# Decay products of the two widest levels as one 128-column product per head, and 128-row products for the low-rank gate, in a hybrid decoder step

## The chip, the core and the metric

The kernel runs on one core of a Trainium2 chip. A core has five engines that work in parallel: TensorE (PE, matrix products; its weight loads are listed as PEld), VectorE (DVE), ScalarE (ACT), GpSimd (POOL) and SyncE (SP, here the queue that issues most transfers). Data lies in HBM, is moved by DMA into SBUF (128 partitions), and products land in PSUM, from where VectorE or ScalarE read them. The metric is the device time of one execution in microseconds (us), as the median of several runs. Before the change it is 1834.86 us (three runs, 1833.53 to 1837.37).

## The reference, cut to what matters

One layer of a decoder trunk for a prompt of 256 tokens and 8 single-token samples. A combined input projection feeds three branches: spatial gating (A), a gated linear recurrence of 8 heads (B, "HGRN2") and one of 4 heads (C, "GLA"). They are merged, projected, and followed by an MLP. Both recurrences are computed by the same function; the decays of C come from a projection of rank 16:

```python
def step(S, inp):
    qc, kc, vc, lc = inp
    b = jnp.cumsum(lc, axis=1)
    diff = b[:, :, None] - b[:, None, :]
    decay = jnp.exp(jnp.where(causal, diff, -jnp.inf))
    att = jnp.einsum('bthd,bshd,btshd->bhts', qc, kc, decay)
    o = jnp.einsum('bhts,bshv->bthv', att, vc) + ...

log_a = jax.nn.log_sigmoid(glr @ p['gla_w_up'][l] + p['gla_b_up'][l]) / GLA_TAU
```

So `att[t, s]`, for s before t, is a sum over the 128 channels d of q[t,d] k[s,d] exp(b[t,d] - b[s,d]), where b is the running sum of the log decays. `glr` has 16 columns, `gla_w_up` is 16 by 512.

## The kernel before

**The main stream.** Nearly all of TensorE's work is the projections. `linear` (L716) runs `granule` (L649) over the weight's row blocks: 512 KB of weights are loaded by SyncE (L616), split by ScalarE into a rounded high part (`whi`, L109) and by VectorE into the rest (`wlo`, L106), and each 128 by 128 block is used in three products, L659, L660 and L661, with 264 columns (256 prompt tokens and 8 samples). The split runs two blocks ahead, into six buffers.

**The background.** The mixers' own work is cut into steps by Python generators (`mixer_a`, `mixer_r`, `samples_r`). After each granule `background` (L699) lets them go on by as much as a rate allows; a generator yields after each step, and `yield READY` holds it until the next granule. So TensorE's order, written out by hand in program order, is: 24 main products, then whatever small products the generators have reached. `slot` (L666) collects the products of the narrow levels (L679, 128 small ones at most) and of the samples' states (L686), and the steps of the conditioning projection (L376). The order on VectorE and ScalarE in this part is chosen by the scheduler of the framework.

**The recurrence (`mixer_r`, L1121).** It runs three times, for groups of four heads: twice for B, once for C. For a group, channels lie on partitions and heads and tokens along the free axis: q, k and the running sum c are [128, 4 heads, 264]. Decays are handled by levels: for a level of width m, the tokens are cut in pieces of 2m; within a piece the first half gives the s side and the second half the t side, and exp(b[t] - b[s]) is written as a product of two factors, both relative to the sum at the end of the first half. The levels 16 to 1 go through `slot` in blocks of 32 tokens. The two widest, m = 32 and m = 64, are a loop of their own (L1186). For such a level a tile `e` ([128, 4, 264], from the pool `blkp`) holds the t-side factors in `es` and the s-side factors in `ef`, interleaved as the tokens are. They are made by an exponential (L1192), a subtraction (through the helper at L106), an exponential (L1195) and two multiplications (helper L100). Then, after a `READY`, for each head and each half of the prompt (`hf`, 128 tokens) one product (L1208) takes all 128 columns of `e` in that half as the stationary operand, s side and t side alike, and the 64 t-side columns as the moving one. The result is [128, 8, 64] in one PSUM bank (`sm`). ScalarE then copies the useful blocks into `att` (L1211 and L1212 for m = 32, L1214 for m = 64); `att` is [128, 8, 128], indexed by twice the head plus the half.

After the loop come the products between the two halves (L1232: `kd` and `qd`, four heads, 128 by 128 by 128), transposes (L1239), the new states (L1248, L1249) and the outputs (L1271 to L1274).

**The samples' states (`samples_r`).** POOL issues the loads of the states (L1077) and of broadcast value rows (L1083); ScalarE scales a state (L1103), VectorE adds the new value (L1105), and POOL issues the store (L1106).

**The low-rank gate (`gla_group`, L1029).** A tile `wl` of 16 partitions holds `gla_w_up` (`wup`, 512 columns) and the 16 rows `lr` of the input projection (264 columns). The weights come by a POOL transfer (L1035), `lr` is copied by ScalarE out of the accumulator (L1043), and four products (L1048) with 16 rows each, one after each piece of the value projection, give the gate's inputs; VectorE adds the bias (L1049).

Of the kernel before, what the change touches and what calls it, by code (L numbers as in the profile page):

```python
# [15 lines left out]
P = 128  # L16
D = 2048
KT = D // P
NP = 256
NS = 8  # L20
NT = NP + NS
# [36 lines left out]
def hybrid_step_kernel(  # L58
# [8 lines left out]
    nc = tc.nc  # L67
    V, S, T = nc.vector, nc.scalar, nc.tensor
# [13 lines left out]
    def nm(s):  # L82
        uid[0] += 1
        return f"{s}_{uid[0]}"

    def blk(shape=None, dt=F32):
        shape = shape or [P, 4, NT]
        return blkp.tile(shape, dt, tag="b", name=nm("b"))

    def sm(shape=None):  # L90
        return psm.tile(shape or [P, 512], F32, tag="sm", name=nm("sm"))
# [4 lines left out]
    def const(shape, name, dt=F32):  # L96
        return cp.tile(shape, dt, tag=name, name=name)

    def mul(o, a, b):
        V.tensor_tensor(o, a, b, op=ALU.mult)  # L100

    def add(o, a, b):
        V.tensor_tensor(o, a, b, op=ALU.add)  # L103

    def sub(o, a, b):
        V.tensor_tensor(o, a, b, op=ALU.subtract)  # L106
# [56 lines left out]
    ps = sm()  # L163
# [120 lines left out]
    ps = sm([P, P])  # L284
# [431 lines left out]
    def linear(w, k0, nk, c0, width, xh, xl):  # L716

        acc = new_acc()
        kc = min(nk, 1024 // width)
        for kb in range(0, nk, kc):  # L720
            granule(w, k0, kc, c0, width, [acc], xh, xl, kb, kb == 0, kb + kc == nk)
            background()
        return acc[:, 0:width // P, 0:NT]
# [4 lines left out]
    def pair(b, g):  # L728
        return b[:, 2 * g:2 * g + 2, :]
# [9 lines left out]
    def zin(c0, width=CW):  # L739
        return linear(win, 0, KT, c0, width, hH, hL)  # L740
# [69 lines left out]
    for ci, n in enumerate(CHUNKS):  # L810
# [5 lines left out]
        for gi in range(ng):  # L816
# [5 lines left out]
            for acc, (c0, dst, fn) in zip(accs, begin[gi * gn:gi * gn + gn]):  # L822
                z = acc[:, :, 0:NT]
# [150 lines left out]
    def log_sigmoid(out, z, a):  # L974

        S.activation(a, z, AF.Abs)
        yield
        S.activation(a, a, AF.Exp, scale=-1.0)
        yield 1.6
        S.activation(a, a, AF.Ln, bias=1.0)  # L980
        yield 1.8
        V.scalar_tensor_tensor(out, z, 0.0, a, ALU.min, ALU.subtract)
        yield


    att = const([P, 8, P], "att")
# [42 lines left out]
    def gla_group():  # L1029
        G = Group()  # L1030
        G.dv, G.i = 256, 2
        G.q, G.g, G.k, G.v = blk(), blk(), blk(), [blk(), blk()]
        wl = blk([16, 512 + NT])
        wup, lr = wl[:, 0:512], wl[:, 512:512 + NT]
        nc.gpsimd.dma_start(wup, gla_w_up[0])  # L1035
        for s in range(2):
            z = zin(6144 + s * CW)
            S.copy(pair(G.q, s), z)
        for s in range(2):
            z = zin(6656 + s * CW)  # L1040
            S.activation(pair(G.k, s), z, AF.Copy, scale=GLA_SCALE)
        z = zin(9216, P)
        S.copy(lr, z[0:16, 0, :])  # L1043
        for s in range(4):
            z = zin(7168 + s * CW)
            S.copy(pair(G.v[s // 2], s % 2), z)
            ps = sm()
            T.matmul(ps[:, 0:NT], wup[:, s * P:(s + 1) * P], lr, start=True, stop=True)  # L1048
            V.tensor_scalar(G.g[:, s, :], ps[:, 0:NT], bupT[:, s:s + 1], None, ALU.add)  # L1049
        G.s_in = lambda b, h, n: state_gla[0, b, h:h + n].rearrange("h k v -> k h v")  # L1050
        G.s_out = lambda b, h, n: gla_sample[0, b, h:h + n].rearrange("h k v -> k h v")
        G.p_out = lambda h, n: gla_prompt[0, 0, h:h + n].rearrange("h k v -> k h v")

        def gates():
            yield from log_sigmoid(G.g, G.g, blk())
            V.tensor_scalar(G.g, G.g, 1.0 / GLA_TAU, None, ALU.mult)
            yield

        G.gates = gates
        return G  # L1060
# [60 lines left out]
    def mixer_r(G):  # L1121
# [4 lines left out]
        def v4(b, w):  # L1126
            return b[:, :, 0:NP].rearrange("p h (n j) -> p h n j", j=w)
# [17 lines left out]
        c = g  # L1145
# [13 lines left out]
        for li, m in enumerate(LEVELS):  # L1159
            n = NP // (2 * m)  # L1160
            yield lambda: len(levels) < LEVELS_HELD
            e = blk()
            ev, cv = v4(e, 2 * m), v4(c, 2 * m)
            ef, es = ev[:, :, :, 0:m], ev[:, :, :, m:2 * m]
# [16 lines left out]
        for b in range(4):  # L1181
            r = slice(32 * b, 32 * b + 32)
# [3 lines left out]
        for m in (32, 64):  # L1186
            n = NP // (2 * m)
            e = blk()
            ev, cv = v4(e, 2 * m), v4(c, 2 * m)
            ef, es = ev[:, :, :, 0:m], ev[:, :, :, m:2 * m]  # L1190
            mid = cv[:, :, :, m - 1:m].to_broadcast([P, 4, n, m])
            S.activation(es, cv[:, :, :, m:2 * m], AF.Exp)  # L1192
            sub(ef, mid, cv[:, :, :, 0:m])
            yield
            S.activation(ef, ef, AF.Exp)  # L1195
            mul(es, es, v4(q, 2 * m)[:, :, :, m:2 * m])
            yield
            mul(ef, ef, v4(k, 2 * m)[:, :, :, 0:m])
            add(cv[:, :, :, m:2 * m], cv[:, :, :, m:2 * m], mid)
            yield  # L1200

            yield READY
            ps = sm([P, 8, 64])
            for h in range(4):
                for hf in range(2):
                    b = e[:, h, P * hf:P * hf + P]
                    rhs = b.rearrange("p (n j) -> p n j", j=2 * m)[:, :, m:2 * m]
                    T.matmul(ps[:, 2 * h + hf, :].rearrange("p (n j) -> p n j", j=m), b, rhs, start=True, stop=True)  # L1208
            yield
            if m == 32:  # L1210
                S.copy(att[0:32, :, 32:64], ps[0:32, :, 0:32])  # L1211
                S.copy(att[64:96, :, 96:128], ps[64:96, :, 32:64])  # L1212
            else:
                S.copy(att[0:64, :, 64:128], ps[0:64])  # L1214

        cv = v4(c, P)
        kd, qd = blk([P, 4, NP]), blk([P, 4, P])
# [12 lines left out]
        ps = sm([P, 4, P])  # L1230
# [5 lines left out]
        for hf in range(2):  # L1236
            ps = sm([P, 4, P])
# [27 lines left out]
        for hf in range(2):  # L1265
            for h0 in range(0, 4, nh):
                ps = sm([P, nh, dv])
                for i in range(nh):
                    h = h0 + i
# [7 lines left out]
                for i in range(nh):  # L1277
                    h = h0 + i
# [10 lines left out]
        for j in range(nj):  # L1289
            for h2 in range(2):  # L1290
                ps = sm([P, 2, NP])
# [19 lines left out]
    for i in range(2):  # L1311
        Gs.append(hg_group(i))
        gens.append(mixer_r(Gs[i]))
        bg.g.append(gens[i])
    rate[:] = RATES[0]
    Gs.append(gla_group())
    gens.append(mixer_r(Gs[2]))
    bg.g.append(gens[2])

# [160 lines left out]
    for m in range(8):  # L1480
        if m in PRE_AT:
            n = N_PRE // len(PRE_AT)
            for _ in range(n):
                pre.load(True)
        z = linear(w_out[0], 0, KT, m * CW, CW, mH, mL)
# [29 lines left out]
    ps = sm([P, 2, KT, NS])  # L1515
# [178 lines left out]
    for t in range(2):  # L1694
        for hf in range(2):
# [8 lines left out]
            if t == 0 and hf == 0:  # L1704
# [3 lines left out]
                ps = sm([P, P])  # L1708
# [52 lines left out]
```

## Time and profile before

| what | before |
|---|---|
| median of three runs | 1834.86 us (1833.53 to 1837.37) |
| the profiled execution | 1832.18 us |
| its span, first to last instruction | 1830.4 us |
| mean granted TensorE clock | 0.997 |
| records of TensorE (PE) | 17012 |
| L659, L660, L661 together | 3850.9 us of overlapping durations, 13872 records |
| L1208 | 96 records, 434 to 716 us |
| L1048 | 8 records, 366 to 409 us |
| HBM traffic | 427.60 MB read, 11.70 MB written |

How to read the profile: times are microseconds from the span's start. A product of fp32 operands appears as two PE records and two PEld records, a main product as one of each. A record's duration overlaps that of the next, since matmuls are pipelined; the pace is the distance between starts. In a list of groups, "128\*128 128x64 f32 x96" is the size of the stationary operand, the output and the number of records. In a timeline, a bracket at the end gives the time the engine was idle before the instruction and what released it; "issue" there means that the profile shows nothing that it waited for.

### The profile page before, as it was taken

How to read it: one execution, taken by the hardware profiler on the slowest of the kernel's cores; microseconds unless marked ns; L12 is line 12 of the kernel's file. 1: busy time of each engine (PE TensorE's matmuls, PEld its weight loads, DVE VectorE, ACT ScalarE, POOL GpSimd, SP SyncE). 2: the span in 40 equal slices, each digit the busy share in tenths (PEclk: the TensorE clock that was granted, in tenths of full speed). 3: DMA queues.
4: the chain of work that ended last, by engine and by line, in shares of the span. 5: the costliest groups of instructions: out<-in, count | busy, mean ns of one | idle time of the engine just before them, and what ended most of it. 6: DMA issues, size and time to landing. Idle time of an engine off the chain costs nothing.

```text
span 1830.4 us, 42186 instructions
## 1 busy us (share of the span) xinstructions
PE 1788.7 (98%) x17012; PEld 1696.5 (93%) x17012; DVE 1181.8 (65%) x2092; ACT 1000.3 (55%) x1818; POOL 131.3 (7%) x210
## 2 busy tenths in 40 slices
PE   6999999999999999999999999999999999999998
PEld 4889999989988999989999989999999999999997
DVE  4566677787576696566555667555666666666666
ACT  5544364666755765654445666555554545454544
POOL 4221000111111101210000000000000000000000
PEclk9999999999999999999999999999999999999999
DMA  9999697788787788897987964777666666666663
GB/s 326 354 343 304 195 304 231 215 266 276 239 287 233 229 270 278 274 323 250 308 254 265 327 180 146 246 256 227 191 197 194 197 194 196 195 195 196 196 196 106
DMA packets 330179, 442.05 MB, mean 242 GB/s; under 512 B 14946, under 2 KB 276944, under 8 KB 329984
## 3 DMA queue, kind: packets, MB, share of 16 engines
q1 hardware_dynamic: 311728, 380.26, 65.0%
q0 software_dynamic: 17184, 57.85, 9.1%
q8 instruction: 133, 2.18, 0.5%
q10 hardware_dynamic: 1072, 1.25, 0.2%
q14 instruction: 62, 0.51, 0.1%
HBM read 427.60 MB, written 11.70 MB: 240 GB/s over the span
## 4 chain that ended last, share of the span: by engine, by line
PE 88%; DMA 2%; DVE 2%; issue 1%; ACT 1%; POOL 0%; DVEq 0%; ACTq 0%; POOLq 0%
PE mm L659 27%; PE mm L661 26%; PE mm L660 26%; PE ada L376 3%; DMA vbc<-vs_d 1%; PE ada L308 1%; DVE wlo L106 1%; PE sm L851 1%; PE sm L1208 1%; PE sm L679 1%; PE sm L686 1%; DMA raw<-in_w_in_dram 0%; DVE b L106 0%; PE sm L1578 0%; ACT whi L109 0%
## 5 line engine op out<-in xcount | busy, mean ns | idle before, releaser
L659 PE MATMUL mm<-b,whi 128*128 128x264 f32 x4624 | 1292.4, 279 | 12.3 <-issue 5.1
L661 PE MATMUL mm<-b,wlo 128*128 128x264 f32 x4624 | 1279.7, 277 | 5.1 <-DVE wlo L106 4.5
L660 PE MATMUL mm<-b,whi 128*128 128x264 f32 x4624 | 1278.8, 277 | 0.8 <-DVE b L106 0.7
L106 DVE TENSOR_TENSOR wlo<-raw,whi 128x512 fp32r<-128x512 f32 x1136 | 774.4, 689 | 489.1 <-ACT whi L109 475.0
L109 ACT CAST whi<-raw 128x512 fp32r<-128x512 f32 x1136 | 691.8, 616 | 644.5 <-DVE wlo L106 331.7
L659 PEld LDWEIGHTS mm<-b,whi 128*128 128x128 f32 x4624 | 875.8, 189 | 53.0 <-issue 28.0
L661 PEld LDWEIGHTS mm<-b,wlo 128*128 128x128 f32 x4624 | 876.2, 189 | 7.3 <-DVE wlo L106 7.2
L660 PEld LDWEIGHTS mm<-b,whi 128*128 128x128 f32 x4624 | 876.2, 189 | 4.4 <-issue 3.0
L103 DVE TENSOR_TENSOR b<-b,mm 128x528 f32<-128x528 f32 (+1 forms) x137 | 95.7, 699 | 24.5 <-PE mm L661 13.0
L1105 DVE SCALAR_TENSOR_TENSOR st<-vbc,b,st 128x128 f32<-128x128 f32 (+1 forms) x96 | 34.2, 390 | 55.2 <-DMA vbc<-vs_d 50.4
L1103 ACT ACTIVATE st<-st,fs 128x128 f32<-128x128 f32 (+1 forms) x96 | 37.1, 430 | 50.5 <-DMA st<-in_state_hgrn_dram 26.9
L488 POOL DMA_DIRECT2D b<-in_w_ada_dram x64 | 46.2, 724 | 126.0 <-PE ada L308 94.4
L376 PE MATMUL ada<-araw,cT 128*32 128x512 f32 x296 | 39.8, 601 | 0.0
L308 PE MATMUL ada<-b,cT 128*32 128x256 f32 (+1 forms) x640 | 35.1, 356 | 2.8 <-DMA b<-in_w_ada_dram 2.6
L100 DVE TENSOR_TENSOR b<-b,b 128x512 f32<-128x512 f32 (+1 forms) x47 | 33.9, 741 | 1.3 <-ACT b L1221 1.0
L1106 POOL DMA_DIRECT2D out_dram<-st x32 | 23.6, 736 | 130.5 <-DVE st L1105 130.5
L308 PEld LDWEIGHTS ada<-b,cT 128*32 128x32 f32 x640 | 17.8, 113 | 14.9 <-DMA b<-in_w_ada_dram 6.2
L376 PE MATMUL ada<-b,cT 128*32 128x512 f32 x216 | 26.2, 594 | 0.0
L106 DVE TENSOR_TENSOR b<-gt,b 128x528 fp32r<-128x528 f32 x32 | 22.7, 710 | 3.2
L106 DVE TENSOR_TENSOR b<-b 128x1024 f32<-128x1024 f32 (+1 forms) x24 | 24.3, 1017 | 0.0
L1632 ACT ACTIVATE b<-vt 128x528 fp32r<-128x528 f32 x32 | 23.0, 719 | 1.0
L106 DVE TENSOR_TENSOR b<-b,b 128x1056 fp32r<-128x1056 f32 (+3 forms) x21 | 20.8, 991 | 4.0 <-ACT b L109 3.8
(344 smaller groups left out, 854.0 us busy)
## 6 DMA issues: line engine op xcount, KB each, us to landing
raw<-in_w_in_dram SPq DMA_DIRECT2D x231, 512.0 KB, 4.8
raw<-in_w_mlp_up_dram SPq DMA_DIRECT2D x128, 512.0 KB, 3.9
raw<-in_w_mlp_down_dram SPq DMA_DIRECT2D x128, 512.0 KB, 3.7
araw<-in_w_ada_dram SPq DMA_DIRECT2D x74, 512.0 KB, 5.7
b<-in_w_ada_dram SPq DMA_DIRECT2D x54, 512.0 KB, 6.6
b<-in_w_ada_dram POOLq DMA_DIRECT2D x48, 512.0 KB, 8.9
raw<-in_w_branch_dram SPq DMA_DIRECT2D x48, 512.0 KB, 4.5
raw<-in_w_out_dram SPq DMA_DIRECT2D x32, 512.0 KB, 5.3
```

The source lines that it names most:

```text
L100: V.tensor_tensor(o, a, b, op=ALU.mult)
L103: V.tensor_tensor(o, a, b, op=ALU.add)
L106: V.tensor_tensor(o, a, b, op=ALU.subtract)
L109: S.copy(hi, src)
L308: T.matmul(acc[32 * j:32 * j + 32, 0:n], cT[:, k, :], w[:, n * j:n * j + n], start=k == 0, stop=k == KT - 1)
L376: T.matmul(self.acc[32 * j:32 * j + 32, :], cT[:, k, :], ws[j // 2][:, j % 2 * 512:j % 2 * 512 + 512], start=k == 0, stop=k == KT - 1)
L488: queue.dma_start(w[:, i], w1[k * P:(k + 1) * P, :, self.k0 * P:(self.k0 + self.n) * P])
L659: T.matmul(o, a, xh(k + j), start=first and j == 0, stop=False)
L660: T.matmul(o, a, xl(k + j), start=False, stop=False)
L661: T.matmul(o, b, xh(k + j), start=False, stop=last and j == n - 1)
L1103: S.activation(st[:, i, :], st[:, i, :], AF.Copy, scale=fs[:, h0 + i, b:b + 1])
L1105: V.scalar_tensor_tensor(st[:, i, :], v[:, i, :], k[:, h0 + i, NP + b:NP + b + 1], st[:, i, :], ALU.mult, ALU.add)
```

## The change

In the two widest levels `e` is laid out by role and no longer by token: columns 0 to 127 of a head hold all s-side factors of the 256 tokens, columns 128 to 255 all t-side factors, each in pieces of m. One product per head (L1205 after) then takes the 128 s-side columns as the stationary and the 128 t-side columns as the moving operand, for both halves of the prompt at once. Of its 128 by 128 result the n diagonal blocks of m by m (n = 256 / 2m, four or two) are used, and each is copied into `att` by an instruction of its own (L1210 after) that covers the four heads.

For the gate, `wl` has 128 partitions. POOL first clears it (128 by 776), then issues the load of the weights into the first 16; `lr` is copied into the first 16 partitions. The four products (L1048) are written as before and now have 128 rows, of which 112 are zero.

```diff
-        wl = blk([16, 512 + NT])
+        wl = blk([P, 512 + NT])
         wup, lr = wl[:, 0:512], wl[:, 512:512 + NT]
-        nc.gpsimd.dma_start(wup, gla_w_up[0])
+        nc.gpsimd.memset(wl, 0.0)
+        nc.gpsimd.dma_start(wup[0:16], gla_w_up[0])
...
-        S.copy(lr, z[0:16, 0, :])
+        S.copy(lr[0:16], z[0:16, 0, :])
...
             e = blk()
-            ev, cv = v4(e, 2 * m), v4(c, 2 * m)
-            ef, es = ev[:, :, :, 0:m], ev[:, :, :, m:2 * m]
+            cv = v4(c, 2 * m)
+            ef, es = (e[:, :, a:a + P].rearrange("p h (n j) -> p h n j", j=m) for a in (0, P))
...
-            ps = sm([P, 8, 64])
+            ps = sm([P, 4, P])
             for h in range(4):
-                for hf in range(2):
-                    b = e[:, h, P * hf:P * hf + P]
-                    rhs = b.rearrange("p (n j) -> p n j", j=2 * m)[:, :, m:2 * m]
-                    T.matmul(ps[:, 2 * h + hf, :].rearrange("p (n j) -> p n j", j=m), b, rhs, start=True, stop=True)
-            yield
-            if m == 32:
-                S.copy(att[0:32, :, 32:64], ps[0:32, :, 0:32])
-                S.copy(att[64:96, :, 96:128], ps[64:96, :, 32:64])
-            else:
-                S.copy(att[0:64, :, 64:128], ps[0:64])
+                T.matmul(ps[:, h, :], e[:, h, 0:P], e[:, h, P:NP], start=True, stop=True)
+            yield
+            by_half = att.rearrange("p (h f) t -> p h f t", f=2)
+            for b in range(n):
+                hf, r = 2 * m * b // P, 2 * m * b % P
+                S.copy(by_half[r:r + m, :, hf, r + m:r + 2 * m], ps[m * b:m * b + m, :, m * b:m * b + m])
```

## The prediction

> **What bounds the kernel now.** I read the page's first part, then TensorE's own waits, then the stretch in which the change works (about 340 to 760 us).
>
> ```profile
> PE 1788.7 (98%) x17012; PEld 1696.5 (93%) x17012; DVE 1181.8 (65%) x2092; ACT 1000.3 (55%) x1818; POOL 131.3 (7%) x210
> PE mm L659 <- issue: 5.1, 2, 2.9
> PE mm L661 <- DVE wlo L106: 4.5, 6, 2.3
> 460.00:560.00 100.00, 98.32 (x1100) 90.99 (x1098) 71.41 (x141) 69.82 (x148) 9.72 (x15) 1.00 0.78 254
> ```
>
> The first line gives busy time, share and records; the two waits give total, times and longest; the last line is a stretch with the busy time of PE, PEld, DVE, ACT and POOL, then the granted clock, DMA share and GB/s. TensorE is busy 98% of the span and 98.3% of the stretch where VectorE and ScalarE are fullest (71 and 70%), and its waits are a few us in all. So what leaves TensorE's queue shortens the run, unless a wait takes it back. TensorE's order by source line is unchanged but for the removed products.
>
> **The decay products (L1208).** Six times (three groups, two levels) eight products give way to four of twice the columns.
>
> ```profile
> 434.26 1.89 PE L1208 MATMUL sm<-b 128*128 128x64 f32 x16
> 435.96 0.36 PE L659 MATMUL mm<-b,whi 128*128 128x264 f32 x1
> 436.16 0.28 PE L660 MATMUL mm<-b,whi 128*128 128x264 f32 x1
> ...
> 455.96 1.05 PE L1232 MATMUL sm<-b,b 128*128 128x128 f32 x8
> 456.86 0.27 PE L1239 MATMUL sm<-cst,b 128*128 128x128 f32 x1
> ...
> L1208 PE MATMUL sm<-b x96: 219/275/275, 434.3 to 716.3; 128*128 128x64 f32 x96
> ```
>
> Start, duration, then the line: durations overlap, so I count start to start. Each product is two records (48 products, x96). From 434.26 to 436.16, less the 0.11 us between L659 and L660, sixteen records take 1.79 us: 0.112 each. L1232 is exactly the new form, four products of 128 by 128 by 128: eight records from 455.96 to 456.86, 0.90 us, again 0.112 each. A record of 64 columns thus costs as much as one of 128. Saved: 1.79 - 0.90 = 0.89 us a level, **5.4 us** for six.
>
> [...] That the columns decide after all stays a rival.
>
> **The gate's products (L1048).** Four products of 16 rows, each two records.
>
> ```profile
> 365.56 0.28 PE L661 MATMUL mm<-b,wlo 128*128 128x264 f32 x1
> 365.77 0.71 PE L1048 MATMUL sm<-b 16*128 16x264 f32 x2
> 366.41 0.38 PE L659 MATMUL mm<-b,whi 128*128 128x264 f32 x1
> 366.62 0.28 PE L660 MATMUL mm<-b,whi 128*128 128x264 f32 x1
> ...
> 734.19 0.59 PE L1248 MATMUL sm<-b,b 128*128 128x256 f32 x2
> 734.62 0.59 PE L1249 MATMUL sm<-b,b 128*128 128x256 f32 x2
> ...
> 407.76 1.07 PE L376 MATMUL ada<-araw,cT 128*32 128x512 f32 x8
> ...
> 409.61 0.28 PE L660 MATMUL mm<-b,whi 128*128 128x264 f32 x1
> ...
> 343.50 1.06 PE L376 MATMUL ada<-araw,cT 128*32 128x512 f32 x8
> ...
> 344.71 0.28 PE L660 MATMUL mm<-b,whi 128*128 128x264 f32 x1
> ```
>
> From L661 at 365.56 to L660 at 366.62 is 1.06 us. With full rows it should be 0.11 for L661, 0.45 for the product (L1248's 0.43 us at 256 columns, scaled to 264) and 0.11 for L659: 0.67. Saved 0.39, and the other two that stand between main products alike. The fourth follows L376: 1.85 us from 407.76 to 409.61, against the 1.21 us that L376 to L660 takes without a product between, plus 0.45: 0.19 saved. Sum 3 x 0.39 + 0.19 = **1.4 us**. Bounds 0 (if padding buys nothing) and 1.4.
>
> **What is added.** Nine copies out of PSUM become eighteen smaller ones, and a POOL clear of 128x776 stands ahead of the load of the gate's weights.
>
> ```profile
> L1211 ACT COPY att<-sm x3: 357/362/363, 439.9 to 705.9; 32x256 f32<-32x256 f32 x3
> L1214 ACT COPY att<-sm x3: 566/577/580, 450.2 to 719.3; 64x512 f32<-64x512 f32 x3
> L873 ACT COPY sqs<-sm x3: 250/250/254, 356.8 to 637.3; 32x128 f32<-32x128 f32 x2, 64x128 f32<-64x128 f32 x1
> ...
> L1150 POOL MEMSET a<- x3: 330/338/338, 358.6 to 639.4; 128x256 f32 x3
> 210.99 0.52 POOL L1035 DMA_DIRECT2D b<-in_gla_w_up_dram  x1 [10.73 <-PE ada L308]
> 332.78 0.58 POOL L945 DMA_DIRECT2D out_dram<-sqs  x1 [121.26 <-ACT sqs L944]
> ```
>
> ScalarE: four copies of 128 columns at 0.25 us for two at 0.36 (+0.28), two of 256 at 0.36 for one at 0.58 (+0.15), in three groups 1.3 us. I take 0: in the stretch above ScalarE idles 30% and TensorE waits mostly for nothing of it; without that cover it costs 1.3. In the second group the four copies now stand ahead of the next level's L1195, which then comes about 1 us later, ahead of a product that is only issued some background steps after. The exponentials and multiplications of the levels keep 512 columns an instruction: 0.
>
> The clear is about 0.34 x 776/256 = 1.0 us on POOL; it inherits the wait for L308, the load follows it, and POOL's next work is at 332.78, the first gate product at 365.77. Cost 0; if VectorE had to stand still for all of it, 1.0.
>
> **A loss.** VectorE stood behind a transfer amid the gate's products:
>
> ```profile
> 397.29 0.88 DVE L1105 SCALAR_TENSOR_TENSOR st<-vbc,b,st 128x128 f32<-128x128 f32 x3 [5.10 <-DMA vbc<-vs_d]
> ```
>
> What TensorE wins shortly before, while VectorE stands there, can only become waiting for VectorE's subtractions. I take one gate product's worth, -0.4, between 0 and all of the first three, -1.2.
>
> **TensorE's instruction supply.** Its two "issue" waits are not noise.
>
> ```profile
> q8 instruction: 133, 2.18, 0.5%
> ...
> 0.00:539.19 539.19, 515.98 (x5177) 471.37 (x5178) 367.15 (x713) 305.00 (x560) 78.60 (x123) 1.00 0.83 277
> 0.00:543.62 543.62, 520.41 (x5306) 475.67 (x5306) 369.43 (x717) 307.00 (x563) 78.60 (x123) 1.00 0.83 278
> 0.00:563.02 563.02, 539.57 (x5689) 493.22 (x5690) 386.20 (x747) 318.47 (x586) 81.57 (x128) 1.00 0.83 277
> 0.00:675.90 675.90, 649.47 (x6840) 597.09 (x6840) 467.40 (x900) 392.26 (x741) 96.70 (x150) 0.99 0.82 272
> ...
> 560.00 1.29 PE L679 MATMUL sm<-b 128*32 128x32 f32 x126
> 565.89 0.27 PE L659 MATMUL mm<-b,whi 128*128 128x264 f32 x1 [2.86 <-issue]
> ...
> 672.08 1.32 PE L679 MATMUL sm<-b 128*32 128x32 f32 x128
> 678.16 0.38 PE L659 MATMUL mm<-b,whi 128*128 128x264 f32 x1 [2.19 <-issue]
> ...
> 566.00:570.00 4.00, 4.00 (x23) 4.00 (x23) 2.72 (x6) 3.57 (x9) 0.00 (x0) 0.58 0.69 240
> 679.00:683.00 4.00, 4.00 (x69) 3.95 (x56) 4.00 (x9) 1.75 (x4) 0.00 (x0) 0.57 0.62 190
> ```
>
> The 34,024 PE and PEld records over 133 instruction packets are 256 a packet. Up to the first halt there are 11,379 records, up to the second 13,680: 2,301 apart, 3 less than 9 x 256 (waits also take a place). So both halts are at a packet's edge. Both come after a burst of 128 small L679 products, 256 records in about 1.2 us, where main products take 14 us for a packet. The packet before the first halt began about 49 records into its burst (11,074 records at 560.00), near 560.25, and lasted 2.7 us; with the 2.86 us halt the next was there after 5.6. Before the second: 3.5 + 2.2 = 5.7 us. A packet from 539.19 to 543.62 (257 records) took 4.4 us without a halt. So a packet needs at least 4.4 to 5.7 us (an estimate from these three).
>
> The change takes 16 PE and 16 PEld records to 8 and 8 a level, so edges fall later in the code: by 31 records (32 less one added wait) in the second group's bursts, 62 in the third's. A main record is 0.056 us, a burst's 0.005. The packet of 539.19 gives 31 main records for 31 of the burst: 4.4 - 1.6 = 2.8 us, so a new halt of 1.6 to 2.8. That before 563.02 gains 1.6: 4.3, halt 0.1 to 1.3 instead of 2.9. That before 675.90 takes in six main records and part of the 64-product burst behind: about 4.0, halt 0.4 to 1.7 instead of 2.2. Sum 2.1 to 5.8 against 5.1; I take the middle, 4.0: **1.1 saved**, between -0.7 and +3.0. After each old halt the granted clock fell to 0.58 and 0.57 for 4 us, which costs 1.7 us each; each shorter halt may escape that. I take one of two gone: **1.7 saved**, between -1.7 (three such) and +3.4.
>
> **Sum.** 5.4 + 1.4 - 0.4 + 1.1 + 1.7 = 9.2 us, 0.5%. The profiled execution took 1832.18 us around a span of 1830.4: 1823.0. The runs shown have a median of 1834.86, 2.7 above it, so I state the forecast against the median: 1834.86 - 9.2 = **1825.7**. By the bounds: 5.4 + 1.4 + 3.0 + 3.4 = 13.2 saved gives 1821.7; 5.4 - 1.2 - 0.7 - 1.7 - 1.3 - 1.0 = -0.5 gives 1835.4, all mishaps at once.
>
> **The rivals.**
> 1. *The halts stay as they are* (supply depends on what else is on the queues at the moment: the last transfer share before them is not in my model). Then 5.4 + 1.4 - 0.4 = 6.4 saved: 1828.5. For: the lower bound rests on three packets. Against: 9 x 256.
> 2. *Columns set a product's pace.* No saving on L1208: 9.2 - 5.4 = 3.8, 1831.1. Against: L1232's row.
> 3. *Transfers hold it.* VectorE's and ScalarE's waits for state transfers, like the 5.10 us above, do not move earlier with TensorE, and the first and second group's savings (4 x 0.89) and the gate's become waiting; halts unchanged: 5.4 + 1.4 - 3.6 - 1.4 = 1.8, 1833.1. For: POOL issues those loads after waits on others. Against: these others are TensorE's products themselves, so the loads should move along.
> 4. *Slower: landings fall behind.* The same loads collide with the weight stream at its new position and land later, so that VectorE's subtraction L106 comes too late more often. Price of one: the longest such wait, 2.3 us, and 1.7 for the clock after it, 4.0. It decides from four added waits on: 16 - 9.2 = 6.8 slower, 1841.7. Against: six such waits in the whole run now, 4.5 us together.
> 5. *It doesn't do what it says*: the halves' blocks could need the waits of one another so that no product starts earlier; but each level's product already waits for both halves' exponentials, and TensorE's order keeps its places. No chance of its own.
>
> **How the numbers follow.** Forecast 0.58, rival 1 0.20, rival 2 0.04, rival 3 0.12, rival 4 0.06. The range 1821.5 to 1832.0 holds the forecast's bounds but for the mishaps together, rivals 1 and 2, and little of 3. This measurement tells about 0.2%, 3.7 us, from no change: faster means under 1831.2. Faster: 0.56 of the forecast, 0.20, 0.02 of rival 2 and 0.03 of rival 3, about 0.81; slower 0.06; same 0.13.
>
> **What would show it.** L1205 in six blocks of eight records, 0.90 us each from start to start; the gate's product 0.67 us between its neighbours; PE records 48 fewer; "issue" waits near 541, 562 and 668 us at edges 256 records apart, each under 2.2 us; ACT copies of 0.25 and 0.36 us. It would be wrong if L1205 took 1.8 us, if the halts were at other places or longer, or if PE's waits for wlo and whi grew by what L1208 gave.

## The result and the profile after

| | before | changed |
|---|---|---|
| median of six runs each, first comparison | 1836.4 us (1833.53 to 1839.9) | 1827.16 us (1825.16 to 1832.91) |
| ratio to before, 95% interval | 1 | 0.9958 (0.9946 to 0.997) |
| the same two kernels, second comparison | 1837.1 us, 15 runs | 1826.29 us, 5 runs; 0.9947 (0.9933 to 0.996) |
| the profiled execution | 1832.18 us, span 1830.4 | 1827.14 us, span 1825.4 |

The change is faster by 0.42% by the ratio, which is 7.7 us; the medians of the first comparison are 9.2 us apart. The two profiled executions differ by only 5.0 us: that of before was faster than all its six runs, and that of the changed kernel is at its median.

The page of the changed kernel, its first part:

```profile
PE 1780.2 (98%) x16964; PEld 1690.1 (93%) x16964; DVE 1181.2 (65%) x2092; ACT 1001.2 (55%) x1827; POOL 132.3 (7%) x211
```

TensorE has 48 records fewer, ScalarE nine more, VectorE as many as before; the instruction packets are 133 again. The first product block and the first gate product, in TensorE's timeline of the changed kernel (start, duration, line; the product loop that the prediction calls L1205 is L1206 in this profile, the copies are L1211, the gate's product L1049):

```profile
437.14 1.05 PE L1206 MATMUL sm<-b 128*128 128x128 f32 x8
437.95 0.36 PE L659 MATMUL mm<-b,whi 128*128 128x264 f32 x1
438.15 0.28 PE L660 MATMUL mm<-b,whi 128*128 128x264 f32 x1
...
366.65 0.28 PE L661 MATMUL mm<-b,wlo 128*128 128x264 f32 x1
366.76 0.61 PE L1049 MATMUL sm<-b 128*128 128x264 f32 x2
367.01 0.47 PE L659 MATMUL mm<-b,whi 128*128 128x264 f32 x1
367.32 0.28 PE L660 MATMUL mm<-b,whi 128*128 128x264 f32 x1
```

Counted as in the prediction, the block takes 438.15 - 437.14 - 0.11 = 0.90 us against 1.79, and the gate's product 367.32 - 366.65 = 0.67 us between its neighbours against 1.06. Both are as worked out. The other blocks and gate products agree: four of the six blocks stand ahead of a main product and fall from 1.79 to 0.90 us, the two ahead of L376 from 1.82 to 0.98; three gate products fall from 1.06 to 0.67, the fourth from 1.85 to 1.66. In all TensorE does 5.2 and 1.4 us less.

TensorE's waits in the stretch from 340 to 760 us, before and then after (total, times, longest):

```profile
PE mm L659 <- issue: 5.1, 2, 2.9
PE mm L661 <- DVE wlo L106: 1.6, 3, 0.7
PE mm L659 <- ACT whi L109: 0.3, 1, 0.3
...
```

```profile
PE mm L661 <- DVE wlo L106: 2.4, 4, 0.7
PE sm L679 <- issue: 2.4, 2, 2.1
PE mm L659 <- ACT whi L109: 1.6, 1, 1.6
PE mm L660 <- issue: 1.1, 1, 1.1
PE mm L659 <- ACT gt L1337: 0.8, 1, 0.8
```

The "issue" waits go from 5.1 to 3.5 us, in three pieces where there were two. Waits for VectorE's and ScalarE's halves of the split go from 1.9 to 4.0, and a wait of 0.8 for ScalarE's L1337 (at 715 us) is new. So all waits in this stretch together do not fall: they are 7.2 us before and 8.3 after. Where the three pieces lie, and what the clock does behind the longer two (timeline rows with the idle time in brackets; then stretches with busy times, clock, DMA share and GB/s; then counts up to a halt), in the changed kernel:

```profile
545.50 0.30 PE L679 MATMUL sm<-b 128*32 128x32 f32 x12 [0.33 <-issue]
567.30 0.38 PE L660 MATMUL mm<-b,whi 128*128 128x264 f32 x1 [1.05 <-issue]
675.06 0.53 PE L679 MATMUL sm<-b 128*32 128x32 f32 x36 [2.06 <-issue]
...
567.00:571.00 4.00, 3.69 (x31) 2.82 (x31) 1.51 (x5) 1.97 (x7) 0.00 (x0) 1.00 0.79 282
675.00:679.00 4.00, 3.94 (x67) 3.90 (x68) 4.00 (x9) 2.73 (x6) 0.00 (x0) 1.00 0.73 244
0.00:565.99 565.99, 537.79 (x5689) 493.63 (x5689) 387.99 (x751) 320.47 (x592) 84.01 (x131) 0.99 0.83 277
0.00:672.81 672.81, 643.45 (x6839) 593.01 (x6839) 467.03 (x900) 393.58 (x748) 97.64 (x151) 0.99 0.83 274
```

Up to the second halt there are 11,378 records, up to the third 13,678: one and two fewer than the 11,379 and 13,680 at which the old kernel halted, although 16 records a level are missing in between. The halts stayed at the same counts and so moved to later code. Behind both the clock is now 1.00 in the 4 us in which it had been 0.58 and 0.57.

But it falls at two other places. Two stretches of the changed kernel, behind the waits near 400 and 800 us, then the old kernel behind its own wait near 807 us:

```profile
401.00:405.00 4.00, 3.96 (x21) 3.96 (x22) 3.97 (x8) 3.40 (x7) 0.00 (x0) 0.60 0.71 224
800.00:804.00 4.00, 3.42 (x18) 3.43 (x19) 4.00 (x7) 1.76 (x3) 0.73 (x1) 0.64 0.81 253
...
807.00:811.00 4.00, 3.66 (x33) 3.12 (x34) 4.00 (x8) 1.88 (x4) 0.72 (x1) 1.00 0.72 211
```

The wait near 800 us is for VectorE's L106 and of much the same length as the old one (2.6 and 2.3 us), and yet only one of the two is followed by a low clock. So in this pair the clock gives nothing back: the mean granted clock is 0.997 before and 0.996 after, and the two executions are only 5.0 us apart. Over all runs for which a clock is on record it is 0.9956 before (61 runs) and 0.9964 changed (11 runs). By these means the clock is worth about 1.4 us (an estimate: 0.00075 of 1830 us, from the means before rounding; single runs scatter by 0.006).

### The profile page after: what moved, and what is told of

It is laid out like the page before. It is cut to its first block, busy times and chain, and to the rows that moved or that the text cites. A ratio compares the mean times of both kernels' runs of the same rounds, so it can differ in the third digit from the quotient of the medians.

```text
span 1825.4 us, 42105 instructions
## 1 busy us (share of the span) xinstructions
PE 1780.2 (98%) x16964; PEld 1690.1 (93%) x16964; DVE 1181.2 (65%) x2092; ACT 1001.2 (55%) x1827; POOL 132.3 (7%) x211
## 3 DMA queue, kind: packets, MB, share of 16 engines
q8 instruction: 133, 2.18, 0.5%
## 4 chain that ended last, share of the span: by engine, by line
PE 87%; DMA 2%; DVE 2%; issue 2%; ACT 1%; POOL 0%; DVEq 0%; ACTq 0%; POOLq 0%
PE mm L659 27%; PE mm L661 26%; PE mm L660 26%; PE ada L376 3%; DMA vbc<-vs_d 1%; PE ada L308 1%; DVE wlo L106 1%; PE sm L851 1%; DMA raw<-in_w_in_dram 1%; PE sm L679 1%; PE sm L686 0%; DVE b L106 0%; PE sm L1575 0%; DMA st<-in_state_hgrn_dram 0%; DVE b L100 0%
## 5 line engine op out<-in xcount | busy, mean ns | idle before, releaser
L659 PE MATMUL mm<-b,whi 128*128 128x264 f32 x4624 | 1292.7, 280 | 11.7 <-ACT b L825 3.6
L661 PE MATMUL mm<-b,wlo 128*128 128x264 f32 x4624 | 1279.4, 277 | 5.3 <-DVE wlo L106 5.0
L106 DVE TENSOR_TENSOR wlo<-raw,whi 128x512 fp32r<-128x512 f32 x1136 | 774.5, 690 | 487.7 <-ACT whi L109 475.8
L659 PEld LDWEIGHTS mm<-b,whi 128*128 128x128 f32 x4624 | 876.0, 189 | 53.9 <-issue 26.6
L661 PEld LDWEIGHTS mm<-b,wlo 128*128 128x128 f32 x4624 | 876.0, 189 | 7.1 <-DVE wlo L106 7.1
L376 PE MATMUL ada<-araw,cT 128*32 128x512 f32 x296 | 39.8, 601 | 0.0
L376 PE MATMUL ada<-b,cT 128*32 128x512 f32 x216 | 26.2, 593 | 0.0
L106 DVE TENSOR_TENSOR b<-gt,b 128x528 fp32r<-128x528 f32 x32 | 22.8, 712 | 3.2
L106 DVE TENSOR_TENSOR b<-b 128x1024 f32<-128x1024 f32 (+1 forms) x24 | 24.4, 1019 | 0.0
L106 DVE TENSOR_TENSOR b<-b,b 128x1056 fp32r<-128x1056 f32 (+3 forms) x21 | 20.9, 993 | 4.0 <-ACT b L109 3.9
```

Source lines behind the costliest of these rows:

```text
L376: T.matmul(self.acc[32 * j:32 * j + 32, :], cT[:, k, :], ws[j // 2][:, j % 2 * 512:j % 2 * 512 + 512], start=k == 0, stop=k == KT - 1)
L659: T.matmul(o, a, xh(k + j), start=first and j == 0, stop=False)
L661: T.matmul(o, b, xh(k + j), start=False, stop=last and j == n - 1)
```

## The experiments

My theory: records set a product's pace (5.4 us), the gate's saving is real on TensorE, and the packets' edges decide the halts. Rivals: columns set the pace; the halts come and go with transfers; the copies eat into the gain; the gain is the gate's.

**Each half alone.** The changed kernel with the gate of before, and before with the gate of the changed kernel; in the second:

```diff
-        wl = blk([16, 512 + NT])
+        wl = blk([P, 512 + NT])
...
-        nc.gpsimd.dma_start(wup, gla_w_up[0])
+        nc.gpsimd.memset(wl, 0.0)
+        nc.gpsimd.dma_start(wup[0:16], gla_w_up[0])
...
-        S.copy(lr, z[0:16, 0, :])
+        S.copy(lr[0:16], z[0:16, 0, :])
```

> The products alone; the gate keeps its 16 rows. My theory: the removed records are worth 5.4 us (six levels by 0.89) and the packet edges fall as in the changed kernel, so also 1.5 us of shorter halts and up to 3.4 us of clock: 6 to 10 us below before, and 1.4 us above the changed kernel. Rival (columns set the pace): not below before by more than 4 us. Rival (most of the gain is the gate's): the changed kernel's time less what the gate alone gives.

> The padded gate alone; the products are those of before. My theory: 1.4 us below before (1835.0 if before is 1836.4), the four gate products 0.67 us between their neighbours, halts at the same packet edges as before (near 563 and 676 us) and of the same size. Rival (padding buys nothing, the saving comes from elsewhere): no difference to before.

The products alone took 1828.16 us against 1835.69, ratio 0.9963 (0.9948 to 0.9977), as expected and not to be told from the whole change. The gate alone took 1834.24, ratio 1.0 (0.9989 to 1.001), so it is worth between -1.8 and +2.0 us, and the 1.4 us that I expected can't be told from nothing. Its halts near 567 and 678 us are at the old counts and of 2.3 and 2.6 us, in place of 2.9 and 2.2. Its trace says why little of the saving reaches the end. First the gate alone near 386 us, then TensorE's waits from 380 to 404 us in the products alone, the gate alone and the changed kernel:

```profile
386.44 0.38 PE L661 MATMUL mm<-b,wlo 128*128 128x264 f32 x1 [0.59 <-DVE wlo L106]
```

```profile
PE mm L659 <- ACT whi L109: 0.8, 1, 0.8
PE mm L661 <- DVE wlo L106: 0.5, 1, 0.5
```

```profile
PE mm L661 <- DVE wlo L106: 1.4, 2, 0.8
PE mm L659 <- ACT whi L109: 0.9, 1, 0.9
```

```profile
PE mm L659 <- ACT whi L109: 1.6, 1, 1.6
PE mm L661 <- DVE wlo L106: 1.3, 2, 0.7
```

Without padded rows TensorE waits 0.8 (before) and 1.3 us there, with them 2.3 and 2.9. The wait near 386 us, of 0.58 or 0.59 us, stands in all eight profiled executions with 128 rows and in none of the four with 16 or 32. Behind the waits near 400 us the clock fell in four of the eight, that of the changed kernel above among them (0.60 from 401 to 405 us), and in none of the four (in before 1.00 over the same stretch). VectorE's row in the changed kernel, and the same place before:

```profile
384.14 1.22 DVE L106 TENSOR_TENSOR b<-b 128x1024 f32<-128x1024 f32 x1
385.28 0.68 DVE L106 TENSOR_TENSOR wlo<-raw,whi 128x512 fp32r<-128x512 f32 x1
```

```profile
383.06 1.21 DVE L106 TENSOR_TENSOR b<-b 128x1024 f32<-128x1024 f32 x1
384.20 0.68 DVE L106 TENSOR_TENSOR wlo<-raw,whi 128x512 fp32r<-128x512 f32 x1
```

Both executions run the split right behind a 1.2 us subtraction of the narrow levels. The changed run is 1.09 us later before the first gate product (L661 ahead of it at 366.65, not 365.56), and VectorE is still 1.08 later here. TensorE has saved 0.39 at each of two gate products by then, is only 0.3 later, and catches up with VectorE: the 0.8 us become waiting.

**32 rows in place of 128.**

```diff
-        wl = blk([P, 512 + NT])
+        wl = blk([32, 512 + NT])
```

> The changed kernel with 32 rows in the gate's products, not 128. If the switch between operand sizes is what a 16-row product costs on both sides, 32 rows pay it too: 1.06 us between the neighbouring main products, as with 16 rows. If any padding to a full strip is enough, 0.67 us, as with 128. The time itself moves by less than 1.5 us either way.

One run took 1825.1 us; a single run says nothing on a time this close. The gate's product stands as in before, with 32 rows as with 16:

```profile
366.64 0.28 PE L661 MATMUL mm<-b,wlo 128*128 128x264 f32 x1
366.84 0.71 PE L1049 MATMUL sm<-b 32*128 32x264 f32 x2
367.48 0.38 PE L659 MATMUL mm<-b,whi 128*128 128x264 f32 x1
367.70 0.28 PE L660 MATMUL mm<-b,whi 128*128 128x264 f32 x1
```

1.06 us again. So 32 rows cost as much as 16, and of the three sizes run only the 128 of the neighbours avoids the 0.39 us. The delay lies on both sides: the product starts 0.20 us behind L661 in place of 0.11, and L659 0.64 us behind the product in place of 0.25. These rows do not separate a cost of the change of size from a cost of the smaller product itself.

**Records or columns.** The changed kernel with two products per head of 64 columns each:

```diff
-                T.matmul(ps[:, h, :], e[:, h, 0:P], e[:, h, P:NP], start=True, stop=True)
+                for j in (0, 64):
+                    T.matmul(ps[:, h, j:j + 64], e[:, h, 0:P], e[:, h, P + j:P + j + 64], start=True, stop=True)
```

> The changed kernel with two products of 64 columns per head in place of one of 128, on the new layout, with the new copies: as many records and columns as before in each level, nothing else undone. If records set the pace: sixteen records in 1.79 us a level, 5.4 us more, and the packet edges fall as before, so 2 to 5 us more: 5 to 10 us above the changed kernel, near before. If columns set it: eight records' time, 0.9 us a level, and no more than the edges' 2 to 5 us.

It took 1834.67 us, ratio to before 1.0 (0.9988 to 1.0012): all of the gain is gone, 7.5 us above the changed kernel's 1827.16. Layout, copies and padding are those of the changed kernel. Its block, its first halt, and the clock behind that:

```profile
437.15 1.89 PE L1207 MATMUL sm<-b 128*128 128x64 f32 x16
438.86 0.36 PE L659 MATMUL mm<-b,whi 128*128 128x264 f32 x1
439.05 0.28 PE L660 MATMUL mm<-b,whi 128*128 128x264 f32 x1
...
568.65 0.47 PE L659 MATMUL mm<-b,whi 128*128 128x264 f32 x1 [2.89 <-issue]
...
569.00:573.00 4.00, 4.00 (x23) 4.00 (x23) 2.08 (x5) 3.14 (x8) 0.00 (x0) 0.60 0.59 202
```

Sixteen records take 1.79 us again, the halt is back at 2.89 us, and the clock falls to 0.60.

**The copies.** Each of the 18 issued twice:

> The changed kernel with each of the 18 copies into the attention tile issued twice: 18 more copies, 4.9 us of ScalarE at their medians of 0.26 us. My theory (ScalarE has cover): within 1 us of the changed kernel. Rival (ScalarE's queue is what TensorE waits for here, and the added copies ate part of the gain): 2 to 5 us above it.

1827.66 us, ratio 0.9962 (0.9947 to 0.9976), not to be told from the changed kernel. The intervals alone would leave room for 2 or 3 us, but the trace shows no new wait: TensorE's waits from 340 to 760 us sum to 8.8 us, against 8.3 and 8.8 in the two profiled executions of the changed kernel. ScalarE has cover here.

**Moving the edges.** `slot` was given a count of its bursts, and at chosen ones issues a number of the products of the last level a second time, into the same place with the same values:

```diff
...
+            bursts[0] += 1
+            lhs, rhs = lv[-1][1:3]
+            for r in range(AGAIN.get(bursts[0], 0)):
+                h, hf, b = r // 8, r // 4 % 2, r % 4
+                t0 = hf * P + b * 32
+                T.matmul(pl[32 * b:32 * b + 32, len(lv) - 1, 2 * h + hf, :], lhs[:, h, t0:t0 + 32], rhs[:, h, t0:t0 + 32], start=True, stop=True)
```

Such a product is four records and 0.02 us. In the first run AGAIN is {5: 8} on the changed kernel; in the second {3: 10, 4: 10, 7: 20} on the kernel before; in the third {3: 11, 4: 11, 7: 26} on the changed one.

> The changed kernel, with 8 of the small products of the fifth burst (near 531 us) issued a second time: 32 more records, 0.2 us of work, so that every packet edge behind them falls 32 records earlier, where it fell before the change in the second group. Supply theory: the halt near 566 us grows from 1.3 back to about 3.1 us and the clock falls behind it: 2 to 4 us above the changed kernel, for 0.2 us of work. Rival (halts come and go with transfers, not with edges): within 0.5 us of the changed kernel.

> The kernel before, with 40 small products issued a second time in three bursts (10 near 418, 10 near 425, 20 near 547 us): 160 more records, 0.8 us of work, placed so that the packet edge in the burst near 560 us falls in its middle. Supply theory: the halt near 563 us (3.1 us) and the 1.7 us of lower clock behind it are gone, the one near 676 us stays at about 2: 3 to 4.5 us below before, though the kernel does more work. Rival (halts come and go with transfers): 0.8 us above before.

> The changed kernel with 48 small products issued a second time (11 near 421, 11 near 428, 26 near 549 us): 192 more records, 1.0 us of work, so that the packet edges fall in the middle of the bursts near 545 and 562 us. Supply theory: the halts near 545 (0.5 us) and 566 us (1.3) are gone, that near 672 us stays at about 2.3, so 0 to 1 us below the changed kernel. Rival (halts come with transfers): 1.0 us above it.

The kernel before with 160 records more: 1829.96 us against 1835.69, ratio 0.9975 (0.9964 to 0.9986), by the ratio 4.6 us faster for more work. TensorE's waits from 340 to 760 us, and the clock in the stretch after the old halt, of that run:

```profile
PE sm L681 <- issue: 2.5, 2, 2.3
...
566.00:570.00 4.00, 4.00 (x38) 4.00 (x38) 3.23 (x7) 2.65 (x6) 2.81 (x5) 1.00 0.98 288
```

The halt near 563 us is gone, the one near 676 stays at 2.3, the clock is 1.00 where it was 0.58. The kernel issues the transfers of before, so the rival that the halts come and go with them falls for this halt. It has 134 instruction packets where before has 133, which fits 160 more records at 256 a packet.

The changed kernel with 32 records more took 1829.87 us, ratio 0.9966 (0.9953 to 0.9979): in the direction and of the size expected, though the intervals of 0.9958 and 0.9966 overlap. Its trace is plainer: the halt grew from 1.05 to 2.67 us and the clock behind it is 0.59.

```profile
565.09 0.59 PE L660 MATMUL mm<-b,whi 128*128 128x264 f32 x1 [2.67 <-issue]
...
565.00:569.00 4.00, 3.91 (x21) 3.91 (x22) 1.82 (x4) 2.68 (x6) 0.00 (x0) 0.59 0.71 250
```

The changed kernel with both edges moved took 1827.25 us, ratio 0.9955 (0.9938 to 0.9973): no gain that can be measured. Of its "issue" waits the late one of 2.5 us is left and one of 0.2, but the two that went were short and had kept the clock, and 1.0 us of work was paid for them.

**One level per burst**, to be rid of all three halts:

```diff
-        lv = [x for x in levels if x[0] + AGE <= now[0]][:2]
+        lv = [x for x in levels if x[0] + AGE <= now[0]][:1]
```

> The changed kernel with one narrow level per burst instead of up to two: eighteen bursts of 128 records in place of thirteen, five of them of 256. The work is the same, but five more bursts stand between main products and each pays its change of operand size on both sides, at most the 0.39 us that the 16-row gate product paid: up to 2 us. Supply theory: no packet is used up in under about 6 us, so the halts near 545, 566 and 672 us (0.5, 1.3 and 2.3) are gone: 0 to 4 us below the changed kernel. Rival (halts come with transfers): up to 2 us above it.

> The changed kernel itself, beside the one-level kernel on the same chip: 0.9958 of before within the earlier interval (0.9946 to 0.997); halts near 545, 566 and 672 us again, of 0.5 to 2.7 us, the lower clock behind one of them or none.

A miss: 1833.8 us against 1826.29 for the changed kernel beside it, ratios 0.9989 (0.9978 to 1.0) and 0.9947. The halts are gone, as expected, but TensorE now waits for the others, in the same stretch and just behind it:

```profile
PE mm L659 <- ACT whi L109: 3.3, 2, 2.1
PE mm L661 <- DVE wlo L106: 2.0, 5, 0.6
PE sm L1206 <- DVE b L100: 1.7, 1, 1.7
PE sm L1246 <- ACT b L1249: 1.3, 1, 1.3
...
781.00 0.65 PE L1291 MATMUL sm<-cst,b 128*128 128x128 f32 x4 [3.00 <-ACT b L1293]
```

L1206, L1246 and L1291 now stand in TensorE's queue before their operands are there; that this is because the levels come one slot later, and the products and states behind them too, is an argument and was not tested. I had priced the switches and not the order. From 340 to 830 us TensorE's waits sum to 15.5 us, against 10.9 in either profiled execution of the changed kernel: 4.6 of the 7.5 us. The mean granted clock, 0.9958 against 0.9964, would be about 1 us more (an estimate), and up to 2 were priced for the switches; these two were not separated.

None of the versions beats the changed kernel by more than the noise.

## Why the prediction was right, and where it was off

- *Decay products, 5.4 us*: right; the six blocks add up to 5.2. Going back to 64 columns, all else kept, restored the 1.79 us a block and gave the whole gain back, 7.5 us, where the columns' rival allowed 2 to 5.
- *Gate, 1.4 us, less a loss of 0.4*: the saving on TensorE is right, the loss was mis-sized. I looked for it at the wait for the transfer near 398 us, where a part of it is; the other part lies near 386 us, where VectorE was about to become the bound without showing a wait. The two places cost the gate kernels about 1.5 us more waiting than the others, so all of it is given back. That is more than the upper bound of the loss in the text (1.2 us).
- *Supply, 1.1 us*: right in mechanism, and in the sum. The halts came at the old counts and so in later code, as the 31 and 62 records say. Three halts near 541, 562 and 668 us were forecast at 4.0 us together, where there had been 5.1. "Issue" waits of 0.3, 1.1 and 2.1 us came near 545, 566 and 673 us, 3.5 in all; another execution of the changed kernel had 0.9, 0.6 and 2.8, 4.3 in all. The single sizes are not right. The new halt should have been 1.6 to 2.8 us and was under 1; the last should have shrunk from 2.2 to between 0.4 and 1.7 and did not shrink. That the sum came out is luck: the two errors cancel.
- *Clock, 1.7 us*: about right in size, and not shown beyond noise. Both stretches that the text counted, at 0.58 and 0.57, are gone, which alone would be 3.4 us, but in the profiled execution two others, near 402 and 802 us, at 0.60 and 0.64, took their place. The term looked only behind halts of supply, while these two stand behind waits for VectorE and ScalarE (1.6 and 0.7 us near 400, 2.6 us near 800). The means over all runs say about 1.4.
- *Sum, 9.2 us*: the medians of the first comparison differ by 9.2, but an agreement to the tenth is luck. TensorE does 6.6 us less; what the supply halts gave, 1.6, went into other waits, so that the waits in the stretch rose by 1.1; the clock gave some 1.4. That makes about 7, beside the ratio's 7.7, whose interval is 5.5 to 9.9.
- *Copies and clear, nothing*: right; doubled copies cost nothing measurable. The clear took 0.74 us on POOL at 211.8 us and delayed nothing that shows.
- *Rivals*: that columns decide and that landings make it slower did not happen. That the halts stay as they are is refuted by the traces alone: its 1828.5 us lies as near to the measured 1827.16 as the forecast's 1825.7. That transfers and VectorE hold it is right for the gate alone; of the products a wait of 0.8 us at 715 us may have taken a part back.

## What to carry to other kernels

Read the cost of a small product from the distance between starts in this stream: here a record costs 0.112 us whether 64 or 128 columns follow the load, so half the number of products took half the time (0.90 us a level in place of 1.79), and a product of 16 or 32 rows between main products of 128 costs 0.39 us more than one padded to 128. Here a saving on the bounding engine counted only as far as the next place where its feeder was already at its limit (VectorE near 386 us, 0.59 us of waiting in the gate alone where before had none), and that feeder showed no wait beforehand: its own queue has to be read. "Issue" waits that keep their place when counted in records, and not in code, were the instruction supply here, and 160 small records more ahead of a dense burst moved the time by 4.6 us, more than half of what the edit itself did. Look for low clock over the whole run and over several executions, and not only at the places that the edit touches: here it went at two (0.58 and 0.57 before) and came at two others (0.60 and 0.64).

## What the runs showed of the hardware that was not expected

TensorE's instructions arrived in packets of 256 records (133 packets for 34,024 records; 2.18 MB, so 16.4 KB each), and a burst of small products could use one up before the next was there. A packet that took 4.4 us passed without a halt; one that lasted 2.7 us was followed by a halt of 2.9. The halts of 0.26 us and more lay at the same count modulo 256, from 110 to 115, in all eleven profiled executions that had them. The places missing between them are waits for semaphores in TensorE's own queue, as the prediction takes them: before has three between its halts (at 570.8, 605.1 and 622.7 us), and 2,301 records and 3 waits are 9 x 256; the changed kernel has four between those near 567 and 675 us (568.9 to 619.0 us), with 2,300 records.

Halts of 2.67, 2.86 and 2.89 us near 566 us were followed by some 4 us at a granted clock of 0.59, 0.58 and 0.60, and those of up to 2.3 us there were not. Near 675 us the length does not decide. First the second execution of the changed kernel, then the kernel with doubled copies:

```profile
675.55 0.53 PE L679 MATMUL sm<-b 128*32 128x32 f32 x36 [2.83 <-issue]
676.00:680.00 4.00, 4.00 (x40) 4.00 (x36) 4.00 (x9) 1.77 (x4) 0.00 (x0) 1.00 0.67 221
...
677.53 0.51 PE L679 MATMUL sm<-b 128*32 128x32 f32 x36 [2.07 <-issue]
678.00:682.00 4.00, 4.00 (x25) 4.00 (x23) 4.00 (x9) 2.58 (x6) 0.00 (x0) 0.62 0.70 227
```

So the loss behind a halt, 1.7 us (an estimate, from 4 us at 0.57), was in before nearly as large as the halt of 2.19 us near 676 us, and the longer halt of 2.83 us had none. What decides it these runs do not show.
